# Single-column norm roots, grouped decay exponentials and separate value turning in a two-model block kernel

## The chip, the cores and the metric

The kernel runs on one core of a Trainium2 chip. The metric is the device time of one execution in microseconds. An execution of before is compared with one of after on the same inputs. Five engines work side by side: TensorE (PE, with its weight loads as PEld), VectorE (DVE), ScalarE (ACT), GpSimd (POOL) and SyncE (SP), which only issues DMAs here. Each takes its instructions in order from its own queue and waits at the head of the queue for semaphores of the others.

## The reference, cut to what matters

The program computes two blocks of two layers each on a sequence of 256 tokens, width 1024. The change touches the first layer's gated delta rule and the RMS norms in front of the layers.

```python
def rms_norm(x, gain):
    y = xf * lax.rsqrt(jnp.mean(xf * xf, axis=-1, keepdims=True) + NORM_EPS)
    return (y * gain)

def gdn_mixer(h, ...):
    proj = h @ w_in                      # q, k, v (4096 columns), z (2048), b, a (16 each)
    qkv = silu(causal_dwconv(qkv, conv_w))
    q, k = l2_norm(q), l2_norm(k)        # 8 heads of 128, each used by two of 16 value heads
    g = -exp(a_log) * softplus(a + dt_bias)
    o = gated_delta_rule(q, k, v, g, sigmoid(b))
    o = o * rsqrt(mean(o * o)) * out_gain * silu(z)
    return o @ w_out

# in gated_delta_rule, g summed up inside chunks:
    decay = where(tril, exp(g_i - g_j), 0)
    t_inv = inverse of (eye + strict lower part of k_beta k^T * decay)
    q_dec, k_dec = q * exp(g), k * exp(g_last - g)
```

## The kernel before

The program is unrolled and goes through stages: the gated delta rule (`gdn`, the first 330 us), a feed-forward layer, the second mixer, a second feed-forward layer, then the second model's two mixers and feed-forward layers. Each projection takes 512 KB chunks of weights. A chunk is loaded (`raw`, SP), split by ScalarE into a high part `wh` (a cast, L464) and by GpSimd or VectorE into the rest `wl` (a subtraction of `raw` and `wh`, L467 on GpSimd, L469 on VectorE; the letters P and V of `PLAN` say which, chunk by chunk). Three matmuls then stand for one exact product: `wh` with the high and the low part of the activations (L480, L492, L493) and `wl` with the high part (L483, L494). There are three slots for `raw` and three for `wh` and `wl`, so a chunk can't be prepared before the one three places ahead is done.

What order an engine's queue has is fixed ahead of time by the framework: it gives each instruction the rank that it has in the program, and lays out the queues by rank and by its own estimate of when operands are there. `issue_after(i)` puts the instructions of a block that run on i's engine behind i in that engine's queue, without a wait of its own.

**Norms.** `stats` (L547) sums the squares of a 128-token half by two ScalarE activations into two columns, and calls `rsqrt` (L496), which finds the root by an integer seed and three Newton steps on VectorE. For one column that is nine instructions: v (L505), seed (L509), -v/2 (L514), and three times t = (hv * y) * y (L517) and y = (t + 1.5) * y (L521); L505, L517 and L521 are `scalar_tensor_tensor`, with two tensor inputs in SBUF. `_norm` (L580 on) then makes the scaled rows (L582, `xn`, in the first norm `UU`: x times `rstd` times the row of gains), turns them by TensorE (L592, `ps_t`), and splits them into `h_hi` (L595, ScalarE) and `h_lo` (L596, VectorE). `stats` runs 14 times, twice in front of each of seven norms. The first norm stands at the start of the program, beside the first three weight chunks of z (`g_z`).

**Gated delta rule** (`_gdn_core`). In this order in the program: z of group 0 (`gates(0)`), the 32 columns b and a (`ps_ba`), the decays `gc` as cumulative sums and their turned copy `gcol` by TensorE (L840, L841), `gc` out to DRAM and back as `row`, broadcast over 128 partitions. Then `project` runs k's eight heads in four steps (`kp`) and q's in four (`qp`): per head 24 matmuls into `ps_g`, a causal convolution (`conv_silu`: ScalarE copy L738, three VectorE taps L740, Silu L741), a square `sq` (L868), and TensorE sums of the squares into `pss` (L855). After k's four steps the decays' differences are taken on VectorE (`ekd` L884, `GT` L886, 128x2048 each for two halves n), masked on GpSimd (L887) and exponentiated on ScalarE (L885, L888, L889). ScalarE holds the tables of one set of functions; between Exp and Silu the program has an `ACT_TABLE_LOAD`. Then k's roots (`rsqrt_p`), their turned copy `rrow` (L904) through DRAM into `row` again, the product with `GT` (L916), the matrix `UU` from `ps_kk` (L921 to L927), its diagonal blocks through DRAM into `sA`, and the triangular inverse of these on VectorE (`tri_inverse`, L1849 and L1850, 62 steps), whose result goes through DRAM into `TR`. Beside it the values' first group is projected.

What follows runs by a list of parts, `order`: v is a group of four value heads (`values`: project, convolve; then turn by TensorE, L965, `ps_v`, and multiply by beta, L966, into `vb`), z a group of gates, l the last two levels of the inverse, s the scan over the two halves with the output norm (`out_norm`, L1066 to L1072); parts with a plus run interleaved. The output projection starts beside s3.

Of the kernel before, what the change touches and what calls it, by code (L numbers as in the profile page):

```python
# [11 lines left out]
F32 = mybir.dt.float32  # L12
# [9 lines left out]
S = 256  # L22
# [19 lines left out]
        gk=4,  # L42
        order='v0 z1 v1 z2 l0 v2 l1+s0 v3 l2+s1 z3 l3+s2 s3',
# [337 lines left out]
class Prog:  # L381
    def __init__(self, ctx, tc, ap):
        self.tc, self.nc, self.ap = tc, tc.nc, ap
        nc = self.nc
        self.const = ctx.enter_context(tc.tile_pool(name="const", bufs=1, reuse_waits="tile"))
        self.xp = ctx.enter_context(tc.tile_pool(name="xp", bufs=1, reuse_waits="tile"))
        self.raw = ctx.enter_context(tc.tile_pool(name="raw", bufs=RAWB, reuse_waits="tile"))
        self.wsp = ctx.enter_context(tc.tile_pool(name="wsp", bufs=WSB, reuse_waits="tile"))
        self.hp = ctx.enter_context(tc.tile_pool(name="hp", bufs=1, reuse_waits="tile"))
        self.sm = ctx.enter_context(tc.tile_pool(name="sm", bufs=3, reuse_waits="tile"))  # L390
        self.pa = ctx.enter_context(tc.tile_pool(name="pa", bufs=4, space=PSUM, reuse_waits="tile"))
        self.dr = ctx.enter_context(tc.tile_pool(name="dr", bufs=1, space=DRAM))
# [8 lines left out]
        self.ada_held = None  # L401
        self.spare = []
# [69 lines left out]
    def mm3_a(self, ps, w, kt, width, m0, m, x):  # L472

        nc = self.nc
        (wh, wl), (xh, xl) = w, x
        n = 0
        last = 3 * kt - 1
        for k in range(kt):
            for xx in (xh, xl):
                nc.tensor.matmul(ps, wh[:, k * width + m0 : k * width + m0 + m], xx[:, k, :], start=(n == 0), stop=(n == last))  # L480
                n += 1
        for k in range(kt):
            nc.tensor.matmul(ps, wl[:, k * width + m0 : k * width + m0 + m], xh[:, k, :], start=False, stop=(n == last))  # L483
            n += 1
# [37 lines left out]

    def rsqrt_p(self, out, ws, n, eps, pool):
# [23 lines left out]
    def stats(self, x, t, junk):  # L547
# [6 lines left out]
        self.rsqrt(rstd, ss, (128, 1), 1.0, 1e-6)  # L554
# [178 lines left out]
    def conv_silu(self, pool, dst, ps, mt):  # L733

        nc = self.nc
        y = pool.tile([128, S], F32, name="cv_y", tag="cv_y", bufs=2)
        w = lambda i: self.fcol("convw", mt * 4 + i, 1)
        nc.scalar.activation(y, ps, AF.Copy, scale=w(3))  # L738
        for j in (1, 2, 3):
            nc.vector.scalar_tensor_tensor(y[:, j:], ps[:, : S - j], w(3 - j), y[:, j:], op0=ALU.mult, op1=ALU.add)  # L740
        self.last_conv = nc.scalar.activation(dst, y, AF.Silu)  # L741
# [19 lines left out]
    def _gdn_core(self, x, dr, gi, vb, rq, zs, inner):  # L761
# [42 lines left out]

        run(gates(0))
# [9 lines left out]
        with tc.tile_pool(name="g_r", bufs=1, reuse_waits="tile") as pr:  # L815
# [11 lines left out]
            na = pr.tile([16, 1], F32, name="na")  # L827
            nc.scalar.activation(na, self.fcol("alog", p1=16), AF.Exp)
            nc.vector.tensor_scalar(e, e, na, -1.0, op0=ALU.mult, op1=ALU.mult)
            on = self.one[0:16].to_broadcast([16, 128])  # L830
            gc = rt("gc")
# [5 lines left out]
            ps = self.pm.tile([128, 2, 2, 16], F32, name="ps_bg", tag="mm")  # L837
            for n in range(2):
                sl = slice(n * 128, n * 128 + 128)
                nc.tensor.transpose(ps[:, 0, n, :], beta[:, sl], self.ident[0:16, 0:16])  # L840
                nc.tensor.transpose(ps[:, 1, n, :], gc[:, sl], self.ident[0:16, 0:16])  # L841
            nc.vector.tensor_copy(cols, ps[:, 0])
            nc.vector.tensor_copy(gcol, ps[:, 1])
        sel = self.fcol("sel").rearrange("p (k m) -> p k m", k=8)

        def project(dst, c0, mt0, pool, tag):
# [11 lines left out]
            for c in range(4):  # L858
# [5 lines left out]
                for j in range(2):  # L864
# [3 lines left out]
                    nc.scalar.activation(sq, dst[:, k, :], AF.Square)  # L868
# [5 lines left out]
        with tc.tile_pool(name="g_rk", bufs=1, reuse_waits="tile") as pr:  # L874
            rrow = pr.tile([16, S], F32, name="rrow")
            kp, qp = project(kc, 0, 8, pe, "e"), project(qc, 4, 0, self.pm, "mm")
            for _ in range(self.plan["gk"]):
                next(kp)
            for n in range(2):
                row = pA.tile([128, 16, 128], F32, name="row", tag="row", bufs=2)  # L880
                nc.sync.dma_start(row, dg[:, n * 128 : n * 128 + 128].partition_broadcast(128))
                with tc.issue_after(self.last_conv.ins):
                    if n == 0:
                        nc.vector.tensor_tensor(ekd, row[:, :, 127], gcol[:, 0], op=ALU.subtract)  # L884
                        nc.scalar.activation(ekd, ekd, AF.Exp)  # L885
# [4 lines left out]
            for _ in range(4 - self.plan["gk"]):  # L890
                next(kp)
            next(qp)
            with tc.issue_after(self.last_raw.ins):
# [54 lines left out]

        def values(g):

            vt = []
            for c in range(2):
                ps = self.pa.tile([128, 2, S], F32, name="ps_g", tag="acc")
                v2 = gi.tile([128, 2, S], F32, name="v2", tag="v2", bufs=2)
# [6 lines left out]
                yield  # L961
            for n in range(2):
# [111 lines left out]
        G = dict(v=lambda g: values(g) if g else v0, l=levels, s=scan, z=gates)  # L1074
# [1175 lines left out]
```

## Time and profile before

| | us |
|---|---|
| median of three runs | 1586.95 (1583.37 to 1590.54) |
| profiled execution | 1586.77 |
| its span in the trace | 1585.1 |
| TensorE busy | 1452.5 (92%) |
| VectorE busy | 1124.0 (71%) |
| ScalarE busy | 817.5 (52%) |
| GpSimd busy | 663.6 (42%) |
| mean granted TensorE clock | 0.975 |

The span runs from the first to the last instruction of the trace; the profiled execution's time is 1.7 us more. A wait is the idle time of an engine in front of an instruction, named by what released it last. The granted clock is given as a share of 2.4 GHz. A matmul's duration in the trace is longer than the step to the next one, since they are pipelined. The trace's timeline merges neighbours of one kind: "x8" is eight instructions, with the time from the first one's start to the last one's end.

### The profile page before, as it was taken

To read this page: it belongs to the slowest core of one execution; us is meant where nothing else is said; L and a number is where in the kernel's file an instruction comes from. 1 tells how busy PE (TensorE), PEld (TensorE's weight loads), DVE (VectorE), ACT (ScalarE), POOL (GpSimd) and SP (SyncE) were. 2 spreads that over 40 slices of the span, in tenths; PEclk is the share of its full clock that TensorE was granted. 3 is DMA by queue.
4 is the path that set the end of the run, shared out by engine and by line. 5 is a ranking of instruction groups with operands and counts; after the bars stand their busy time and mean duration, and the time that the engine had idled before them with its cause. 6 is when DMAs were issued, how large, how long until landed. Compare 5 with 4: busy or idle time off the path is not lost.

```text
span 1585.1 us, 25794 instructions
## 1 busy us (share of the span) xinstructions
PE 1452.5 (92%) x9586; PEld 1285.2 (81%) x9586; DVE 1124.0 (71%) x2352; ACT 817.5 (52%) x1479; POOL 663.6 (42%) x433
## 2 busy tenths in 40 slices
PE   5788988999999899999998899898899889899998
PEld 4787877789988787999877676898887777589987
DVE  4567676769666766898476597799975768776652
ACT  4765544445343564554245475455444547466651
POOL 4445732236454241544136413266535521335630
PEclk9899999999999999999999999999999999999999
DMA  4555531478776454888533413777774441375551
GB/s 163 171 169 164 173 104 44 155 257 299 278 294 226 131 183 149 318 326 327 209 118 122 127 54 127 250 266 253 264 260 142 124 129 61 104 250 177 195 189 38
DMA packets 103246, 292.96 MB, mean 185 GB/s; under 512 B 28072, under 2 KB 37968, under 8 KB 96976
## 3 DMA queue, kind: packets, MB, share of 16 engines
q1 hardware_dynamic: 93872, 237.12, 44.3%
q10 hardware_dynamic: 8896, 53.14, 9.3%
q8 instruction: 75, 1.23, 0.3%
q0 software_dynamic: 352, 1.06, 0.2%
q14 instruction: 51, 0.42, 0.1%
HBM read 288.04 MB, written 3.24 MB: 184 GB/s over the span
## 4 chain that ended last, share of the span: by engine, by line
PE 50%; DVE 17%; DMA 5%; issue 4%; ACT 3%; POOL 2%; SPq 0%; ACTq 0%; DVEq 0%; POOLq 0%
PE ps_gu L480 13%; PE ps_gu L483 6%; PE ps_o L493 6%; PE ps_o L494 6%; PE ps_o L492 6%; DVE wl L469 4%; DVE ada_raw L1372 2%; DMA ada_raw<-in_ada 1%; DVE gu_u L2204 1%; ACT wh L464 1%; DMA raw<-in_u_gu 1%; POOL wl L467 1%; PE ps_u L480 1%; DVE rs_t L519 1%; PE ps_bs L1953 1%
## 5 line engine op out<-in xcount | busy, mean ns | idle before, releaser
L467 POOL TENSOR_TENSOR wl<-raw,wh 128x1024 fp32r<-128x1024 f32 (+4 forms) x162 | 403.6, 2498 | 425.6 <-ACT wh L464 344.3
L464 ACT CAST wh<-raw 128x1024 fp32r<-128x1024 f32 (+3 forms) x421 | 423.3, 1018 | 241.1 <-PE ps_o L493 91.1
L469 DVE TENSOR_TENSOR wl<-raw,wh 128x1024 fp32r<-128x1024 f32 (+2 forms) x259 | 347.6, 1352 | 134.4 <-ACT wh L464 132.6
L480 PE MATMUL ps_gu<-h_hi,wh 128*128 128x256 f32 x1280 | 312.6, 283 | 10.3 <-DVE gu_u L2204 10.3
L480 PE MATMUL ps_gu<-h_lo,wh 128*128 128x256 f32 x1280 | 312.0, 282 | 0.0
L480 PEld LDWEIGHTS ps_gu<-h_hi,wh 128*128 128x128 f32 x1280 | 244.2, 191 | 11.3 <-issue 9.0
L480 PEld LDWEIGHTS ps_gu<-h_lo,wh 128*128 128x128 f32 x1280 | 244.3, 191 | 0.2
L1372 DVE CUSTOM_DVE_ANT_0 ada_raw<-ada_raw,ada_cond 128x1024 f32<-128x1024 f32 x96 | 173.6, 1823 | 54.6 <-DMA ada_raw<-in_ada 54.5
L483 PE MATMUL ps_gu<-h_hi,wl 128*128 128x256 f32 x1280 | 178.5, 282 | 1.5 <-POOL wl L467 1.5
L483 PEld LDWEIGHTS ps_gu<-h_hi,wl 128*128 128x128 f32 x1280 | 163.7, 191 | 1.8 <-POOL wl L467 1.7
L494 PE MATMUL ps_o<-wl,act_h 128*128 128x512 f32 x352 | 139.0, 395 | 0.8 <-DVE wl L469 0.5
L493 PE MATMUL ps_o<-wh,act_l 128*128 128x512 f32 x352 | 138.6, 394 | 0.0
L492 PE MATMUL ps_o<-wh,act_h 128*128 128x512 f32 x352 | 138.4, 393 | 0.0
L2204 DVE SCALAR_TENSOR_TENSOR gu_u<-ps_gu,f2s,gu_u 128x254 f32<-128x254 f32 (+1 forms) x176 | 80.9, 477 | 41.2 <-ACT gu_u L2202 39.2
L725 POOL TENSOR_TENSOR act_l<-gu_t,act_h 128x256 fp32r<-128x256 f32 x44 | 55.6, 1267 | 112.8 <-ACT act_h L724 110.9
L2207 POOL TENSOR_TENSOR gu_t<-gu_t,gu_u 128x256 f32<-128x256 f32 x44 | 47.2, 1074 | 90.4 <-DVE gu_u L2204 87.0
L494 PEld LDWEIGHTS ps_o<-wl,act_h 128*128 128x128 f32 x352 | 66.1, 188 | 16.9 <-DVE wl L469 0.9
L493 PEld LDWEIGHTS ps_o<-wh,act_l 128*128 128x128 f32 x352 | 66.1, 188 | 15.1 <-issue 0.2
L492 PEld LDWEIGHTS ps_o<-wh,act_h 128*128 128x128 f32 x352 | 66.1, 188 | 14.9 <-issue 0.2
L2208 ACT CAST act_h<-gu_t 128x256 fp32r<-128x256 f32 x44 | 17.9, 407 | 101.9 <-POOL gu_t L2207 101.8
L740 DVE SCALAR_TENSOR_TENSOR cv_y<-ps_g,fi,cv_y 128x253 f32<-128x253 f32 (+2 forms) x96 | 44.9, 477 | 34.4 <-ACT cv_y L738 33.1
L480 PE MATMUL ps_g<-h_hi,wh 128*128 128x256 f32 x256 | 68.8, 301 | 0.0
(660 smaller groups left out, 3001.6 us busy)
## 6 DMA issues: line engine op xcount, KB each, us to landing
ada_raw<-in_ada ACTq DMA_DIRECT2D x48, 1024.0 KB, 6.3
raw<-in_f_gu SPq DMA_DIRECT2D x88, 512.0 KB, 4.6
raw<-in_u_gu SPq DMA_DIRECT2D x88, 512.0 KB, 4.3
raw<-in_f_dn SPq DMA_DIRECT2D x44, 512.0 KB, 4.7
raw<-in_u_dn SPq DMA_DIRECT2D x44, 512.0 KB, 4.2
raw<-in_g_qkv SPq DMA_DIRECT2D x32, 512.0 KB, 4.0
raw<-in_g_z SPq DMA_DIRECT2D x16, 512.0 KB, 4.0
raw<-in_g_out SPq DMA_DIRECT2D x16, 512.0 KB, 3.5
```

Of the source, the lines that this page charges most:

```text
L464: self.last_copy = nc.scalar.copy(wh[:, :cols], raw[:, :cols])
L467: nc.gpsimd.tensor_tensor(wl[:, :cols], raw[:, :cols], wh[:, :cols].bitcast(F32), op=ALU.subtract)
L469: nc.vector.tensor_tensor(wl[:, :cols], raw[:, :cols], wh[:, :cols].bitcast(F32), op=ALU.subtract)
L480: nc.tensor.matmul(ps, wh[:, k * width + m0 : k * width + m0 + m], xx[:, k, :], start=(n == 0), stop=(n == last))
L483: nc.tensor.matmul(ps, wl[:, k * width + m0 : k * width + m0 + m], xh[:, k, :], start=False, stop=(n == last))
L492: nc.tensor.matmul(ps, xh, wh[:, sl], start=start, stop=False, **kw)
L493: nc.tensor.matmul(ps, xl, wh[:, sl], start=False, stop=False, **kw)
L494: nc.tensor.matmul(ps, xh, wl[:, sl], start=False, stop=stop, **kw)
L725: nc.gpsimd.tensor_tensor(al[:, m, :], t, ah[:, m, :].bitcast(F32), op=ALU.subtract)
L1372: nc.vector.tensor_tensor_reduce(raw[:, j], raw[:, j], self.cond, 1.0, 0.0, op0=ALU.mult, op1=ALU.add, accum_out=mod[:, i : i + 1])
L2204: nc.vector.scalar_tensor_tensor(u[:, j, d:], ps[:, j, : S - d], cw[:, 3 * q + 2 - d : 3 * q + 3 - d], u[:, j, d:], op0=ALU.mult, op1=ALU.add)
L2207: nc.gpsimd.tensor_tensor(t, t, u[:, 0], op=ALU.mult)
```

## The change

It does three things. A new helper, `rsqrt_1`, replaces `rsqrt` in `stats`: the same nine steps, each a `tensor_scalar` with one tensor input, one column wide, whose other operands are one-column scalars per partition in SBUF. In the gated delta rule the turned decays are made after k's first step, the differences of the decays stand behind k's last convolution tap in VectorE's queue, and the exponentials `eg`, `ekd` and both `GT` stand together on ScalarE behind the last square of q's first step; later Silus of `conv_silu` stand behind them. The exponential of A_log moves to the front, and `gc` to a longer-lived buffer. Last, `values` is cut into `values` and `turned`, which `order` places one or more parts later; the buffers `v2` go from two to four.

```diff
-        gk=4,
-        order='v0 z1 v1 z2 l0 v2 l1+s0 v3 l2+s1 z3 l3+s2 s3',
+        order='v0 z1 t0 v1 z2 t1 l0 v2 l1+s0 t2 v3 l2+s1 t3 z3 l3+s2 s3',
...
+    def rsqrt_1(self, out, a, b, eps):
+        V = self.nc.vector
+        v, hv, t = (self.sm.tile([128, 1], F32, name=f"rs_{n}", tag=f"rs1_{n}") for n in "vht")
+        V.tensor_scalar(v, a, b, eps, op0=ALU.add, op1=ALU.add)
+        V.tensor_scalar(hv, v, -0.5, None, op0=ALU.mult)
+        seed = self.sm.tile([128, 1], I32, name="rs_s", tag="rs1")
+        V.tensor_scalar(seed, v.bitcast(I32), -0.5, float(0x5F3759DF), op0=ALU.mult, op1=ALU.add)
+        y = seed.bitcast(F32)
+        for i in range(3):
+            V.tensor_scalar(t, hv, y, y, op0=ALU.mult, op1=ALU.mult)
+            V.tensor_scalar(out if i == 2 else y, t, 1.5, y, op0=ALU.add, op1=ALU.mult)
...
-        self.rsqrt(rstd, ss, (128, 1), 1.0, 1e-6)
+        self.rsqrt_1(rstd, ss[:, 0:1], ss[:, 1:2], 1e-6)
...
-            nc.vector.scalar_tensor_tensor(y[:, j:], ps[:, : S - j], w(3 - j), y[:, j:], op0=ALU.mult, op1=ALU.add)
-        self.last_conv = nc.scalar.activation(dst, y, AF.Silu)
+            self.last_tap = nc.vector.scalar_tensor_tensor(y[:, j:], ps[:, : S - j], w(3 - j), y[:, j:], op0=ALU.mult, op1=ALU.add)
+        with self.tc.issue_after(self.behind.ins) if self.behind else ExitStack():
+            nc.scalar.activation(dst, y, AF.Silu)
...
+        na = gi.tile([16, 1], F32, name="na")
+        nc.scalar.activation(na, self.fcol("alog", p1=16), AF.Exp)
         run(gates(0))
...
-            gc = rt("gc")
+            gc = pA.tile([16, S], F32, name="gc")
...
             kp, qp = project(kc, 0, 8, pe, "e"), project(qc, 4, 0, self.pm, "mm")
-            for _ in range(self.plan["gk"]):
+            next(kp)
+            ps = self.pm.tile([128, 2, 2, 16], F32, name="ps_bg", tag="mm")
+            with tc.issue_after(self.last_mm.ins):
+                for n in range(2):
...
+                    nc.tensor.transpose(ps[:, 0, n, :], beta[:, sl], self.ident[0:16, 0:16])
+                    nc.tensor.transpose(ps[:, 1, n, :], gc[:, sl], self.ident[0:16, 0:16])
+            nc.vector.tensor_copy(cols, ps[:, 0])
+            nc.vector.tensor_copy(gcol, ps[:, 1])
+            for _ in range(3):
                 next(kp)
             for n in range(2):
                 row = pA.tile([128, 16, 128], F32, name="row", tag="row", bufs=2)
                 nc.sync.dma_start(row, dg[:, n * 128 : n * 128 + 128].partition_broadcast(128))
-                with tc.issue_after(self.last_conv.ins):
+                with tc.issue_after(self.last_tap.ins):
                     if n == 0:
                         nc.vector.tensor_tensor(ekd, row[:, :, 127], gcol[:, 0], op=ALU.subtract)
-                        nc.scalar.activation(ekd, ekd, AF.Exp)
                     nc.vector.tensor_tensor(GT[n], row, gcol[:, n].unsqueeze(2).to_broadcast([128, 16, 128]), op=ALU.subtract)
                 nc.gpsimd.affine_select(GT[n], GT[n], [[0, 16], [1, 128]], ALU.is_ge, -1e30, base=0, channel_multiplier=-1)
-                nc.scalar.activation(GT[n], GT[n], AF.Exp)
-            nc.scalar.activation(eg, gcol[:, 1], AF.Exp)
...
             next(qp)
+            with tc.issue_after(self.last_sq.ins):
+                nc.scalar.activation(eg, gcol[:, 1], AF.Exp)
+                nc.scalar.activation(ekd, ekd, AF.Exp)
+                for n in range(2):
+                    self.behind = nc.scalar.activation(GT[n], GT[n], AF.Exp)
...
         def values(g):
-            vt = []
+            vt = vts[g] = []
             for c in range(2):
...
-                v2 = gi.tile([128, 2, S], F32, name="v2", tag="v2", bufs=2)
+                v2 = gi.tile([128, 2, S], F32, name="v2", tag="v2", bufs=4)
...
                 vt.append(v2)
                 yield
+        def turned(g):
+            vt = vts.pop(g)
             for n in range(2):
                 ps = self.pm.tile([128, 4, 128], F32, name="ps_v", tag="mm")
```

## Rows read from the trace of the kernel before

**Rows 1.** Waits of TensorE, 0 to 330 us: total, times, longest (us).
```profile
PE pss L855 <- ACT sq L868: 8.1, 3, 5.3
PE ps_z L493 <- DVE h_lo L596: 6.9, 2, 6.7
PE ps_v L965 <- ACT v L741: 5.8, 3, 4.1
...
PE ps_kk L921 <- ACT kc L741: 1.8, 1, 1.8
...
PE ps_e L1723 <- DMA TR<-dTR: 1.2, 1, 1.2
```
**Rows 2.** Ten-us windows: length, busy (instructions) by engine, granted clock, DMA share, GB/s.
```profile
50.00:60.00 10.00, 10.00 (x88) 10.00 (x86) 7.03 (x10) 7.16 (x13) 7.54 (x3) 1.00 1.08 323
...
70.00:80.00 10.00, 4.66 (x22) 4.55 (x22) 3.78 (x9) 9.91 (x14) 2.47 (x2) 0.50 0.00 0
```
**Rows 3.** Timeline of VectorE: start, us, what, [idle before, releaser].
```profile
10.31 2.35 DVE L521 SCALAR_TENSOR_TENSOR rs_s<-rs_t,rs_s 128x1 f32<-128x1 f32 x1
...
17.75 0.75 DVE L582 SCALAR_TENSOR_TENSOR UU<-x_t,rstd,row 128x512 f32<-128x512 f32 x1
18.41 0.68 DVE L596 TENSOR_TENSOR h_lo<-ps_t,h_hi 128x512 fp32r<-128x512 f32 x1
...
148.31 0.69 DVE L966 TENSOR_TENSOR vb<-ps_v,bcol 128x512 f32<-128x512 f32 x1 [2.11 <-PE ps_v L965]
...
216.90 5.47 DVE L1072 SCALAR_TENSOR_TENSOR zs<-zs,g_rs,vb 128x128 f32<-128x128 f32 x4
```
**Rows 4.** Timeline of GpSimd, two places.
```profile
10.01 7.24 POOL L467 TENSOR_TENSOR wl<-raw,wh 128x1024 fp32r<-128x1024 f32 x3 [8.62 <-ACT wh L464]
...
953.77 0.64 POOL L1823 TENSOR_TENSOR a_Y<-a_Y,lay 128x256 f32<-128x256 f32 x1 [4.77 <-DVE rs_v L507]
```
**Rows 5.** Two lines of the code: count, ns min/median/max, first and last start (us).
```profile
L740 DVE SCALAR_TENSOR_TENSOR cv_y<-ps_g,fi,cv_y x96: 410/481/484, 46.9 to 228.3; 128x255 f32<-128x255 f32 x32, 128x254 f32<-128x254 f32 x32, 128x253 f32<-128x253 f32 x32
...
L517 DVE SCALAR_TENSOR_TENSOR rs_t<-rs_h,rs_s x54: 205/219/2260, 7.5 to 1390.7; 128x1 f32<-128x1 f32 x54
```
**Rows 6.** Timeline of VectorE, three places beside GpSimd's work.
```profile
279.87 2.25 DVE L509 TENSOR_SCALAR rs_s<-rs_v 128x4 int32<-128x4 int32 x1
...
332.75 3.58 DVE L582 SCALAR_TENSOR_TENSOR xn<-x_t,rstd,row 128x512 f32<-128x512 f32 x2
...
954.06 0.14 DVE L509 TENSOR_SCALAR rs_s<-rs_v 128x1 int32<-128x1 int32 x1
```
**Rows 7.** Timeline of TensorE.
```profile
19.15 0.80 PE L493 MATMUL ps_z<-wh,h_lo 128*128 128x512 f32 x1 [6.67 <-DVE h_lo L596]
...
24.55 1.03 PE L592 MATMUL ps_t<-ident,UU 128*128 128x128 f32 x8
...
77.58 0.56 PE L480 MATMUL ps_g<-h_hi,wh 128*128 128x256 f32 x1
...
86.07 0.51 PE L855 MATMUL pss<-fi,sq 128*128 128x16 f32 x4
```
**Rows 8.** Timeline of ScalarE around the exponentials.
```profile
64.95 1.91 ACT L888 ACTIVATE GT<-GT 128x2048 f32<-128x2048 f32 x1 [3.15 <-POOL GT L887]
66.88 1.28 ACT L741 ACT_TABLE_LOAD   x1
68.18 0.72 ACT L741 ACTIVATE kc<-cv_y 128x256 f32<-128x256 f32 x2
```
**Rows 9.** Timeline: a difference on VectorE, the two masks on GpSimd.
```profile
58.97 4.09 DVE L886 TENSOR_TENSOR GT<-row,gcol 128x2048 f32<-128x2048 f32 x1
...
60.86 6.02 POOL L887 TENSOR_SCALAR_AFFINE_SELECT GT<-GT 128x2048 f32<-128x2048 f32 x2
```
**Rows 10.** Timeline: the copy of rrow, its product with GT.
```profile
93.27 0.36 ACT L904 COPY rrow<-ps_rk 16x256 f32<-16x256 f32 x1 [1.20 <-PE ps_rk L903]
...
103.52 2.29 DVE L916 TENSOR_TENSOR row<-GT,row 128x2048 f32<-128x2048 f32 x1 [2.04 <-DMA row<-db]
```

More of the change, by code (lines that the diff above doesn't have):

```diff
@@ L401, in __init__ @@
         self.ada_held = None
+        self.behind = None
         self.spare = []
@@ L482, in mm3_a @@
         for k in range(kt):
-            nc.tensor.matmul(ps, wl[:, k * width + m0 : k * width + m0 + m], xh[:, k, :], start=False, stop=(n == last))
+            self.last_mm = nc.tensor.matmul(ps, wl[:, k * width + m0 : k * width + m0 + m], xh[:, k, :], start=False, stop=(n == last))
             n += 1
@@ L826, in _gdn_core @@
             nc.vector.scalar_tensor_tensor(e, xa, 0.0, e, op0=ALU.max, op1=ALU.add)
-            na = pr.tile([16, 1], F32, name="na")
-            nc.scalar.activation(na, self.fcol("alog", p1=16), AF.Exp)
             nc.vector.tensor_scalar(e, e, na, -1.0, op0=ALU.mult, op1=ALU.mult)
             on = self.one[0:16].to_broadcast([16, 128])
-            gc = rt("gc")
+            gc = pA.tile([16, S], F32, name="gc")
             for n in range(2):
@@ L836, in _gdn_core @@
             nc.sync.dma_start(dg, gc)
[L837 to L843, printed above, removed]
         sel = self.fcol("sel").rearrange("p (k m) -> p k m", k=8)
@@ L867, in project @@
                     sq = gi.tile([128, S], F32, name="sq", tag="sq", bufs=2)
-                    nc.scalar.activation(sq, dst[:, k, :], AF.Square)
+                    self.last_sq = nc.scalar.activation(sq, dst[:, k, :], AF.Square)
                     sqs.append((k, sq))
@@ L876, in _gdn_core @@
             kp, qp = project(kc, 0, 8, pe, "e"), project(qc, 4, 0, self.pm, "mm")
-            for _ in range(self.plan["gk"]):
+            next(kp)
+            ps = self.pm.tile([128, 2, 2, 16], F32, name="ps_bg", tag="mm")
+            with tc.issue_after(self.last_mm.ins):
+                for n in range(2):
+                    sl = slice(n * 128, n * 128 + 128)
+                    nc.tensor.transpose(ps[:, 0, n, :], beta[:, sl], self.ident[0:16, 0:16])
[3 more added lines that the diff above has]
+            for _ in range(3):
                 next(kp)
@@ L881, in _gdn_core @@
                 nc.sync.dma_start(row, dg[:, n * 128 : n * 128 + 128].partition_broadcast(128))
-                with tc.issue_after(self.last_conv.ins):
+                with tc.issue_after(self.last_tap.ins):
                     if n == 0:
                         nc.vector.tensor_tensor(ekd, row[:, :, 127], gcol[:, 0], op=ALU.subtract)
-                        nc.scalar.activation(ekd, ekd, AF.Exp)
                     nc.vector.tensor_tensor(GT[n], row, gcol[:, n].unsqueeze(2).to_broadcast([128, 16, 128]), op=ALU.subtract)
                 nc.gpsimd.affine_select(GT[n], GT[n], [[0, 16], [1, 128]], ALU.is_ge, -1e30, base=0, channel_multiplier=-1)
-                nc.scalar.activation(GT[n], GT[n], AF.Exp)
-            nc.scalar.activation(eg, gcol[:, 1], AF.Exp)
-            for _ in range(4 - self.plan["gk"]):
-                next(kp)
             next(qp)
+            with tc.issue_after(self.last_sq.ins):
[3 more added lines that the diff above has]
+                    self.behind = nc.scalar.activation(GT[n], GT[n], AF.Exp)
             with tc.issue_after(self.last_raw.ins):
@@ L947, in _gdn_core @@
             nc.sync.dma_start(dTR[1], A.rearrange("p c j -> p (c j)"))
+        vts = {}
         def values(g):
-            vt = []
+            vt = vts[g] = []
             for c in range(2):
                 ps = self.pa.tile([128, 2, S], F32, name="ps_g", tag="acc")
-                v2 = gi.tile([128, 2, S], F32, name="v2", tag="v2", bufs=2)
+                v2 = gi.tile([128, 2, S], F32, name="v2", tag="v2", bufs=4)
                 for j in range(2):
@@ L1072, in out_norm @@
                     nc.vector.scalar_tensor_tensor(zs[n][g][:, u, :], zs[n][g][:, u, :], rs[:, u : u + 1], o[:, u, :], op0=ALU.mult, op1=ALU.mult)
-        G = dict(v=lambda g: values(g) if g else v0, l=levels, s=scan, z=gates)
+        G = dict(v=lambda g: values(g) if g else v0, t=turned, l=levels, s=scan, z=gates)
         *first, last = self.plan["order"].split()
```

## The prediction

> **What bounds the kernel now.** The page's busy times come first (the table above): TensorE works nearly throughout, so time can be won only where it stands idle or runs at its lower clock. The diff touches the gated-delta-rule stage (the first 330 us) and the norm roots of all stages. For that stretch I read the waits of TensorE, sorted by their sum [rows 1], then ten-us windows [rows 2] to see what a wait costs afterwards: in 50 to 60 us TensorE is busy throughout at clock 1.00 (2.4 GHz) with 88 matmuls, in 70 to 80 us for 4.66 us with 22, and its granted clock is 0.50 (1.2 GHz). Three waits belong to the three parts of the change: 6.9 us for h_lo of the first norm, 8.1 us for the squares sq (longest 5.3), 5.8 us for v (longest 4.1). Last, I read the queues of the other engines around each of the three, to see what ends the wait.
>
> **Part 1, the roots.** In the first norm VectorE's one-column root steps, normally about 0.22 us for the slower kind [rows 5], take up to 2.35 us: the step at 10.31, and two like it at 12.70 and 15.00 [rows 3]. Each ends when one of the three GpSimd subtractions that begin at 10.01 (2.4 us apiece) ends [rows 4]. They have two tensor inputs in SBUF. Behind them in VectorE's queue stand UU (17.75) and h_lo (18.41), and TensorE waits for h_lo. The new steps read one tensor; the rest are per-partition scalars. Does a one-input step wait? The 96 convolution taps, one input in PSUM, one in SBUF and a scalar, never took over 0.484 us [rows 5], though GpSimd subtracts beside many; a one-column tensor_scalar at 954.06 took 0.14 us in the middle of a GpSimd tensor_tensor (953.77 to 954.41) [rows 4, 6]. The same op on four columns took 2.25 us at 279.87 [rows 6], so columns matter, and the new ones are single.
>
> The Trainium skill, "SBUF — State Buffer", section "Who interferes with whom", speaks against this part: tensor_scalar may enter a mode that takes the port shared with GpSimd, and is then blocked for a whole instruction. The row at 279.87 agrees for four columns, the one at 954.06 does not for one. By the rule alone part 1 would be worth nothing (second rival).
>
> What is late next: the two remaining UU steps (x times rstd times row, two SBUF inputs) wait as before; such a pair took 3.58 us beside GpSimd at 332.75, 1.5 when free [rows 6]. So: five steps of about 0.2 end at 11.4 instead of 17.7; UU waits for the first subtraction (12.6) and ends at 13.4; h_lo's first half (0.68) at 14.1, against 19.1. The second UU waits for the second subtraction (13.4 + 2.4 = 15.8), h_lo's second half ends at 17.2, the third subtraction at 16.5 + 2.4 = 18.9. TensorE restarts at 14.1 instead of 19.15, needs that third split from about 18, and finishes its last four matmuls at 19.8 instead of 24.55 [rows 7]: **4.7 us**. Ends: 2.3 (one more subtraction, 2.4 us, in the way) and 6 (UU does not wait). Everything behind it is a chain from h_lo (z, ba, decays, weights by slots), so it moves as a whole. The other twelve roots run the same number of steps, nine; with 0.14 to 0.22 us for one [rows 5, 6] each changes by -0.3 to +0.2 us: I take 0, ends -3 and +2 for all. The early exponential of A_log is one short activation moved ahead in ScalarE's queue; taken at 0, with up to 1 us if it waits for its DMA in front of a cast.
>
> **Part 2, the exponentials.** Now each GT exponential (1.91 us) sits between k's activations with a table load of 1.28 us on either side (one stands in the rows), and the first waits 3.15 us for GpSimd's mask [rows 8]. The squares come late, TensorE waits, then works at the low clock. What goes: the 5.3 us wait for sq and the 1.8 us for kc [rows 1], and the low clock behind them: q's first pair, 48 matmuls, takes from 77.58 to 86.07, 8.5 us [rows 7], where 88 matmuls, a few small sums among them, fill 10 us at full clock [rows 2], so about 5.8 for 48 with their sums; 2.7 us too much. Together 9.8 us by 86.07. Five of ten table loads between 36 and 91 us go too (6.4 us of ScalarE), covered there by TensorE's work.
>
> What comes: after q's first pair ScalarE does load, eg, ekd, GT twice, load: 1.28 + 0.4 + 3.8 + 1.28 = 6.8 us in one piece. Queued behind it are the next Silus, weight casts, and the copy of rrow, for which the whole chain to the triangular inverse waits. q's pair would end at 86.1 - 9.8 = 76.3; its convolution (three taps of 0.48 and three short activations, about 3 us) at 79.3; the exponentials end at 86.1. GT must be there: the subtractions (2.3 us as the equal-sized product in [rows 10], one took 4.09 beside GpSimd) now follow k's last tap (about 68: 76.3 less the pair's 5.8 and the kk products and sums in front) and end at 73 to 76; the masks (3.0 each) at 79 to 82 with a weight split between [rows 9]. So rrow goes from 93.27 to about 86.9, and its product with GT from 103.52 to about 97 [rows 10]: the chain wins **6.4 us**, not 9.8, and TensorE, in order, waits for the rest at kk. Ends: 0 (masks behind two more splits, rrow no earlier) and 9.8. Casts behind the 6.8 us block are covered by three weight slots, each some 2.9 us of matmuls (half of the pair's 5.8); without that cover the block costs up to 4 us, which lies inside these ends. The transposes of the decays behind a named matmul lose a short wait and meet gc, which comes no earlier: 0.
>
> The Trainium skill, "ScalarE: Activation LUTs", section "What ACT_TABLE_LOAD costs", counts a drain of 1.38 us beside each load, 2.66 in all. Here the load at 66.88 begins as the exponential ends, and the next activation starts at 68.18, 1.30 later [rows 8]: no such drain. By the page the block would be 2.8 us longer and the part worth 3.6.
>
> **Part 3, turning apart from projecting.** TensorE's waits for v go (5.8 us), but what stands behind each decides. VectorE waits 2.11 us at 148.31 for ps_v in the middle of the triangular inverse [rows 3], 2.8 us with a second such place; TensorE waits 1.2 us for the inverse's result TR [rows 1]. Both move, so about 1.5 us is won by the first level step. The longest wait, 4.1 us before 226, hides a VectorE stretch: four steps of the output norm took 5.47 us from 216.90 beside GpSimd [rows 3], and the scan behind them starts no earlier; TensorE would do the z matmuls there and miss them later. I take 0 of it, ends 0 and 4. Part 3: **1.5 us**, ends 0 and 5.
>
> **Sum.** 4.7 + 6.4 + 1.5 = 12.6 us off the profiled execution of 1586.77 us (span 1585.1 and 1.7 around it), which lies within 0.2 us of the median of the three runs, 1586.95: **1574.2 us**.
>
> **Rivals.** First, the gain of part 2 is given back: rrow is no earlier because the GT masks stand behind weight splits in GpSimd's queue, and TensorE arrives early at TR and waits. For it: TensorE already waits 1.2 us there. Against: q's end moves the inverse too. It gives 1586.8 - 4.7 = 1582. Second, the new one-column steps wait for GpSimd as the old ones: 1586.8 - 7.9 = 1578.9; only the rule speaks for it. Third, all covers hold: 6 + 9.8 + 5 = 20.8, 1566. Fourth, slower: between 200 and 300 us the output norms' two-input and four-column steps meet GpSimd's splits, each meeting worth 2.25 us [rows 6]; I count ten now. The shifted order can meet more often. If part 2 is also lost, three more meetings use up part 1's 4.7, and six make it slower by 13.5 - 4.7 = 8.8: 1595.6. For it: nothing orders these engines against each other. Against: six more on ten is much for an unchanged stretch.
>
> **How the numbers follow.** Forecast 0.57, rivals 0.20, 0.05, 0.12 and 0.06. Within 0.5% means 7.9 us, about what a measurement of this kernel can tell from no change, so from 1578.8 on it is no change. Faster: 0.53 of the forecast, the third rival, half of the second: 0.68. Slower: the fourth and a little: 0.07. Same: 0.25. The range goes from the third rival's 1566 to 1584, which takes in the first rival; the slow case and both tails, under 0.2, stay out.
>
> **What would show it.** Right: no one-column root step over 0.3 us near 10 us and TensorE back at its matmuls at about 14; no wait for sq over 2 us and clock 1.00 between 60 and 90; five table loads there; rrow some 11 us earlier (both parts); no wait for v. Wrong: 2.3 us steps left at 10 us; ScalarE idle in front of the GT exponentials with casts behind it; a longer wait for TR; a longer stretch from TR to the end of the stage.

## The result, and the profile after

| | before | after |
|---|---|---|
| median, four runs each side by side (us) | 1585.89 (1583.37 to 1590.54) | 1563.95 (1560.75 to 1570.74) |
| profiled execution | 1586.77 | 1570.74 |
| its span | 1585.1 | 1569.0 |
| first level step (ps_e) starts | 190.21 | 188.16 |
| last output product of the first stage starts | 326.06 | 301.10 |

A level step is a matmul of the inverse's last two levels; the first one (`ps_e`) needs the inverse's result TR. The last output product is the last matmul of the first stage's output projection (`ps_o`).

The change is faster: ratio 0.9866, 95% interval 0.9841 to 0.9891, some 21 us. The forecast of 1574.2 and its range from 1566 to 1584 were too high. The profiled execution of after took the longest of its four, so its trace shows only 16.1 us of the gain. In the traces 25 us are won by the end of the first stage, 18.1 are left when the next stage's gate-up matmuls begin (343.53 before, 325.43 after), 16.1 at the end.

The waits of TensorE in the first 330 us of after (us in total, times, longest):
```profile
PE ps_t L605 <- DVE UU L595: 11.9, 2, 10.0
PE ps_t L605 <- DVE xn L595: 5.6, 3, 2.1
PE ps_z L493 <- DVE h_lo L609: 4.8, 2, 4.6
PE ps_bg L891 <- DVE gc L848: 3.1, 1, 3.1
...
PE ps_e L1745 <- DMA TR<-dTR: 0.5, 1, 0.5
```
The waits for sq, kc and v of [rows 1] are gone. The wait for h_lo has shrunk to 4.6 us, but one for UU of 1.8 has appeared ahead of it (the 10.0 is the program's start), and the next norm's xn costs 5.6 (2.0 in before, from 326 to 346 us).

Windows of after (length; busy us and instructions of PE, PEld, DVE, ACT and POOL; granted clock; DMA share and GB/s):
```profile
36.00:100.00 64.00, 59.25 (x461) 58.21 (x459) 40.95 (x70) 43.80 (x75) 39.54 (x16) 0.92 0.62 195
100.00:190.00 90.00, 87.65 (x607) 80.31 (x605) 75.02 (x163) 53.25 (x102) 65.38 (x31) 1.00 0.67 201
...
70.00:80.00 10.00, 10.00 (x87) 10.00 (x87) 9.89 (x9) 5.13 (x10) 6.77 (x3) 1.00 0.50 158
```
The same windows of before:
```profile
36.00:100.00 64.00, 52.17 (x386) 50.86 (x385) 34.41 (x64) 46.53 (x75) 34.56 (x14) 0.87 0.55 171
100.00:190.00 90.00, 80.36 (x550) 73.99 (x548) 65.74 (x151) 47.13 (x88) 53.31 (x27) 0.96 0.60 179
```
From 70 to 80 us TensorE is now busy throughout at clock 1.00, where [rows 2] has 4.66 us at 0.50. From 36 to 190 us it is busy 14.4 us longer (7.1 + 7.3), at a higher clock.

ScalarE of after, the exponentials together:
```profile
87.48 1.28 ACT L906 ACT_TABLE_LOAD   x1
88.77 0.22 ACT L906 ACTIVATE eg<-gcol 128x16 f32<-128x16 f32 x1
...
89.00 3.69 ACT L909 ACTIVATE GT<-GT 128x2048 f32<-128x2048 f32 x2
92.60 0.34 ACT L921 COPY rrow<-ps_rk 16x256 f32<-16x256 f32 x1
```
The exponentials stand together as forecast, but they begin late (the forecast had the block at 79.3, without part 1), and rrow behind them comes at 92.60 where [rows 10] has 93.27: 0.7 us earlier, not the 11 forecast for both parts together. Part 2 by itself was to bring 6.4 of these; in exps_alone (below) rrow comes at 90.83, 2.4 earlier. The block stands behind q's first squares, which end at 87.46, and these need q's convolution taps. In VectorE's queue the taps stand behind the differences that feed GT, and these met GpSimd's subtractions:
```profile
73.28 2.16 DVE L901 TENSOR_TENSOR ekd<-row,gcol 128x16 f32<-128x16 f32 x1
75.36 6.69 DVE L902 TENSOR_TENSOR GT<-row,gcol 128x2048 f32<-128x2048 f32 x2
81.97 0.47 DVE L753 SCALAR_TENSOR_TENSOR cv_y<-ps_g,fi,cv_y 128x255 f32<-128x255 f32 x1
```
GpSimd's second mask stands behind a weight split, but ends at 88.25, ahead of the first GT exponential at 89.00:
```profile
86.24 2.01 POOL L903 TENSOR_SCALAR_AFFINE_SELECT GT<-GT 128x2048 f32<-128x2048 f32 x1
```
So where do 25 us come from, if the chain to the inverse wins next to nothing? TensorE's projections behind the first level step tell it. Before, from 190.2 to 263 us (count, busy us, mean ns):
```profile
L492 PE MATMUL ps_z<-wh,h_hi 128*128 128x512 f32 x16 | 6.8, 427 | 0.0
L493 PE MATMUL ps_z<-wh,h_lo 128*128 128x512 f32 x16 | 6.8, 426 | 0.0
L494 PE MATMUL ps_z<-wl,h_hi 128*128 128x512 f32 x16 | 6.8, 426 | 0.0
L480 PE MATMUL ps_g<-h_hi,wh 128*128 128x256 f32 x25 | 6.7, 297 | 0.0
L480 PE MATMUL ps_g<-h_lo,wh 128*128 128x256 f32 x26 | 6.7, 286 | 0.0
...
L483 PE MATMUL ps_g<-h_hi,wl 128*128 128x256 f32 x32 | 5.0, 288 | 0.0
```
After, from 188.1 to 240 us; there is no ps_g among them:
```profile
L492 PE MATMUL ps_z<-wh,h_hi 128*128 128x512 f32 x6 | 2.6, 427 | 0.0
L493 PE MATMUL ps_z<-wh,h_lo 128*128 128x512 f32 x6 | 2.5, 410 | 0.0
L494 PE MATMUL ps_z<-wl,h_hi 128*128 128x512 f32 x6 | 2.4, 394 | 0.0
```
Before, 83 products ps_g and 48 ps_z stand behind the first level step; after, 18 ps_z. Undisturbed, 96 ps_g took 11.68 us (152.10 to 163.78 of before), 48 ps_z 11.1 (145.88 to 156.96 of after): 0.12 and 0.23 us each, so 21 us stood behind it and 4 stand there now. From the first to the last level step it takes 72.4 us before, 51.1 after; from there to the end of the stage 63.4 and 61.9.

### The profile page after: what moved, and what is told of

Its sections match the earlier page's. It is cut to its first block, busy times and chain, and to the rows that moved or that the text cites. A ratio compares the mean times of both kernels' runs of the same rounds, so it can differ in the third digit from the quotient of the medians.

```text
span 1569.0 us, 25783 instructions
## 1 busy us (share of the span) xinstructions
PE 1455.1 (93%) x9586; PEld 1286.3 (82%) x9586; DVE 1120.2 (71%) x2352; ACT 811.7 (52%) x1474; POOL 659.3 (42%) x433
## 5 line engine op out<-in xcount | busy, mean ns | idle before, releaser
L469 DVE TENSOR_TENSOR wl<-raw,wh 128x1024 fp32r<-128x1024 f32 (+2 forms) x259 | 356.9, 1385 | 145.2 <-ACT wh L464 143.2
L1394 DVE CUSTOM_DVE_ANT_0 ada_raw<-ada_raw,ada_cond 128x1024 f32<-128x1024 f32 x96 | 160.5, 1685 | 68.7 <-DMA ada_raw<-in_ada 68.7
L738 POOL TENSOR_TENSOR act_l<-gu_t,act_h 128x256 fp32r<-128x256 f32 x44 | 51.8, 1179 | 102.7 <-ACT act_h L737 102.7
L480 PE MATMUL ps_g<-h_lo,wh 128*128 128x256 f32 x256 | 66.2, 293 | 0.0
```

The lines of the kernel that those rows point to most:

```text
L469: nc.vector.tensor_tensor(wl[:, :cols], raw[:, :cols], wh[:, :cols].bitcast(F32), op=ALU.subtract)
L738: nc.gpsimd.tensor_tensor(al[:, m, :], t, ah[:, m, :].bitcast(F32), op=ALU.subtract)
L1394: nc.vector.tensor_tensor_reduce(raw[:, j], raw[:, j], self.cond, 1.0, 0.0, op0=ALU.mult, op1=ALU.add, accum_out=mod[:, i : i + 1])
```

## The experiments

Each was timed in five rounds beside the kernel before. "Left" is the projection work behind the first level step, counted as above; "f0" is the time from the gate-up norm's first xn to that of the next norm, "last" from the last norm's first xn to the end, all from the traces (us).

| kernel | ratio, 95% interval | first level step | left | last output product | f0 | last |
|---|---|---|---|---|---|---|
| before | 1 | 190.2 | 21 | 326.1 | 189.3 | 197.6 |
| after (1+2+3) | 0.9866, 0.9841 to 0.9891 | 188.2 | 4 | 301.1 | 194.2 | 202.7 |
| roots_alone (1) | 1.0025, 1.0006 to 1.0044 | 187.8 | 21 | 323.5 | 192.8 | 200.2 |
| exps_alone (2) | 0.9849, 0.9827 to 0.9871 | 187.7 | 4 | 300.3 | 189.0 | 197.5 |
| turn_alone (3) | 0.9946, 0.9926 to 0.9966 | 188.9 | 22 | 320.0 | 188.5 | 197.5 |
| no_roots (2+3) | 0.9823, 0.9794 to 0.9853 | 186.8 | 4 | 299.1 | 188.2 | 197.5 |
| no_turn (1+2) | 0.9848, 0.9817 to 0.9879 | 188.9 | 4 | 300.8 | 192.3 | 200.6 |
| no_exps (1+3) | 0.9969, 0.9950 to 0.9987 | 184.5 | 22 | 315.7 | 192.4 | 202.7 |
| exps_pure | 0.9840, 0.9818 to 0.9863 | 189.6 | 4 | 304.9 | 188.0 | 197.2 |
| order_alone | 0.9934, 0.9915 to 0.9953 | 215.7 | 0 | 318.8 | 188.1 | 197.4 |
| lo_first | 0.9884, 0.9863 to 0.9904 | 184.4 | 4 | 299.3 | 193.1 | 203.6 |
| first_only | 0.9894, 0.9862 to 0.9926 | 183.3 | 4 | 297.7 | 194.9 | 199.4 |
| roots_rest | 1.0050, 1.0030 to 1.0071 | 190.6 | 21 | 326.5 | 196.0 | 201.2 |
| rest_f0v | 1.0045, 1.0023 to 1.0066 | 189.2 | 21 | 324.9 | 191.4 | 198.7 |
| first_v | 0.9782, 0.9760 to 0.9804 | 182.1 | 4 | 294.9 | 188.2 | 197.3 |
| after_first_v | 0.9830, 0.9802 to 0.9857 | 183.5 | 4 | 296.9 | 193.2 | 200.7 |
| first_v_f0v | 0.9803, 0.9776 to 0.9831 | 182.4 | 4 | 296.7 | 189.1 | 197.2 |

**One part alone, and one part undone.** roots_alone, exps_alone and turn_alone put the change's hunks on the kernel before, one part each; no_roots, no_turn and no_exps leave one out. By their main lines:
```diff
# roots_alone: this alone; no_roots: this undone
-        self.rsqrt(rstd, ss, (128, 1), 1.0, 1e-6)
+        self.rsqrt_1(rstd, ss[:, 0:1], ss[:, 1:2], 1e-6)
# exps_alone / no_exps
-                nc.scalar.activation(GT[n], GT[n], AF.Exp)
...
+            with tc.issue_after(self.last_sq.ins):
# turn_alone / no_turn
-        order='v0 z1 v1 z2 l0 v2 l1+s0 v3 l2+s1 z3 l3+s2 s3',
+        order='v0 z1 t0 v1 z2 t1 l0 v2 l1+s0 t2 v3 l2+s1 t3 z3 l3+s2 s3',
```


> The kernel before with the roots of part 1 alone. Theory: the wait on GpSimd only moves to the two-input UU steps behind the roots, and h_lo of the first half stands behind UU of the second in VectorE's queue, so TensorE restarts at about 19.1 us as before; ratio 1.000, 1584 to 1588 us. Rival, the forecast: TensorE restarts at 14.1 and the kernel gains 4.7 us, about 1581, ratio 0.997.

> The kernel before with part 2 alone (exponentials together, transposes of the decays moved). Theory: projections are a store of work that fills whatever TensorE time is freed ahead of TR, so all of the idle time and half-clock time taken out between 36 and 100 us comes off the end of the stage: about 7 us of idle time and 3 us of clock, some 10 us, 1576 us, ratio 0.9937. Rival: only what brings TR forward counts, and rrow is less than 1 us earlier: 1 to 2 us, 1584. The forecast had 6.4, 1579.5.

> The kernel before with part 3 alone (values turned apart from projecting). Theory of the store of work: TensorE's waits for v (5.8 us) and the half-clock time behind them go and the later scans run without projections between: 7 us, 1579, ratio 0.9956. Rival, the forecast: 1.5 us, 1584.5, ratio 0.999; a second rival is that it gains only where part 2 has freed time: 0, 1586.

> The changed kernel with the old roots (parts 2 and 3 without part 1). If the parts add up (exponentials alone 24 us, turning alone 8.6), 1554 us, ratio 0.979. Theory of the store of work: the exponentials' part has used up the projections that were left behind TR, so turning has nothing more to give: 1559 to 1562, ratio 0.983, TR again near 188 us and the stage's last output product at about 300.

> The changed kernel without part 3 (roots and exponentials). Theory: roots cost 3 to 4 us and turning gives nothing behind the exponentials: 1564 to 1566, ratio 0.987, equal to the changed kernel. Rival, the parts add: 1572, ratio 0.991.

> The changed kernel without part 2 (roots and turning). Both theories: plus 4 and minus 8.6, about 1582, ratio 0.997; the forecast's terms would give 1586.8 - 6.2 = 1580.6.

On the 1587 us of before, the roots alone cost 4 us, the exponentials win 24, the turning wins 8.6. The exponentials alone are worth as much as the whole change. The parts don't add: 28.6 us in sum, 21 together. Turning is worth 8.6 us on before, and about as much on the kernel with the roots (no_exps beside roots_alone), but 4 beside the exponentials (no_roots against exps_alone, intervals overlap) and nothing that can be told in the whole change (no_turn against after). All of the exponentials' expectations were too small, the theory's 10 us too. roots_alone is slower than both of its expectations; its first stage is faster nevertheless, and the loss lies behind it (see the norms below).

**Which piece of part 2.** exps_pure leaves the decays' transposes, gc and the exponential of A_log where they were:
```diff
-        na = gi.tile([16, 1], F32, name="na")
-        nc.scalar.activation(na, self.fcol("alog", p1=16), AF.Exp)
...
-            next(kp)
-            with tc.issue_after(self.last_mm.ins):
...
+            for _ in range(4):
```


> Part 2 with the exponentials together only: the decays' transposes and the exponential of A_log stay where they were. Theory: the exponentials are all of it: 1561 to 1565, ratio 0.985. Rival: the late transposes, which take a TensorE wait out of the stretch, bring a quarter or more: 1568 to 1572, ratio 0.989.

0.9840 beside 0.9849: the place of the exponentials, and of the differences that feed them, is all of it.

**Freed time or order.** With the exponentials together, TensorE's queue has 17 us more projection ahead of the first level step. order_alone puts all 21 us ahead of it without freeing time:
```diff
-        order='v0 z1 v1 z2 l0 v2 l1+s0 v3 l2+s1 z3 l3+s2 s3',
+        order='v0 z1 v1 z2 v2 v3 z3 l0 l1+s0 l2+s1 l3+s2 s3',
...
+        with self.tc.issue_after(behind.ins) if behind else ExitStack():
             for u in range(8):
```


> The kernel before, with only the order of TensorE's work changed: all value and gate projections are issued ahead of the first level step (131 matmuls, some 21 us, stand behind it in the kernel before, 18, some 4 us, in the three kernels with the exponentials together). Theory: it is TensorE's freed time that pays, not the order; without that time the first level step comes at 203 to 210 us, from there to the last level step it takes about 50 instead of 72, and the two cancel: 1582 to 1588, ratio 0.997 to 1.0. Rival: TensorE has room ahead of TR, and the order alone brings most of the 24 us: first level step by 195, 1565 to 1572, ratio 0.988.

Its windows:
```profile
36.00:100.00 64.00, 52.55 (x395) 51.07 (x394) 33.87 (x64) 46.96 (x75) 34.88 (x14) 0.89 0.53 172
100.00:190.00 90.00, 81.90 (x540) 75.92 (x539) 65.53 (x150) 45.43 (x86) 53.27 (x27) 0.92 0.58 178
190.00:215.60 25.60, 24.23 (x155) 21.36 (x155) 12.30 (x23) 12.62 (x21) 16.66 (x8) 1.00 0.63 169
```
Its first level step, which waits for nothing but its queue:
```profile
215.68 0.70 PE L1724 MATMUL ps_e<-TR,UU 128*32 128x32 f32 x32
```
The first level step comes 25.5 us later than before; from it to the last it takes 41.2 us for 72.4. The net, 10.5 us by the ratio (7.3 at the last output product), is more than the theory's 0 to 5 and far from the 24 of the rival. It has a place: TensorE's idle time between first and last level step falls from 10.0 to 4.1 us, and the longest wait for v (4.1) is among what goes. The same stretches of exps_alone:
```profile
36.00:100.00 64.00, 59.30 (x468) 58.39 (x467) 41.66 (x70) 45.46 (x80) 40.53 (x16) 0.95 0.64 197
100.00:187.70 87.70, 84.73 (x583) 76.86 (x582) 69.56 (x156) 48.96 (x90) 61.82 (x30) 1.00 0.67 201
```
From 36 us to its first level step TensorE stands idle for 21.7 us in before, 20.9 in order_alone and 7.7 in exps_alone, at a mean clock of 0.92, 0.92 and 0.98. So the order is worth some 6 to 10 us, about what turning brings alone; the rest of the exponentials' gain needs the freed time.

**The first norm.** lo_first adds one order to the changed kernel; first_only goes back to the old roots in all other norms, too; first_v is no_roots with the stage's first four splits on VectorE, and after_first_v has the new roots as well:
```diff
# lo_first, first_only
+                        with self.tc.issue_after(lo.ins) if t and first else ExitStack():
                             nc.vector.scalar_tensor_tensor(xn[:, hv], ...
# first_v, after_first_v
-        w='PPPVPPPPPVPP...
+        w='VVVVPPPPPVPP...
```


> The changed kernel with one order more: in the first norm the UU steps of the second half of x are issued behind h_lo of the first half. Theory, that the queue order was what kept part 1 from paying: h_lo of the first half ends near 14.5 us, TensorE restarts there instead of 19.05, and 3 to 5 us come off: about 1560 against 1564, ratio to the kernel before 0.9835. Rival: the second half ends later by as much as the first gains, and the projections need both: within 1 us of the changed kernel's 1564.

> The changed kernel with the new roots in the first norm alone, the old ones in the other norms, and UU of the second half of x behind h_lo of the first. Theory: the new roots cost time in the other norms (the first gate-up norm and the last one took some 4 and 5 us longer in each of the three kernels that have them) because the planned order around them shifts; without them there 1567.7 comes down by 8 to 11 us: 1557 to 1560, ratio 0.982. Rival: those 9 us are an accident of when weight splits fall, and the kernel stays within 2 us of 1567.

> Parts 2 and 3 with the old roots, and the first four weight splits of the stage on VectorE instead of GpSimd, so that nothing runs beside the first norm. Theory: the one-column steps take 0.2 us and UU 0.75, TensorE is back at 14 to 15 us instead of 19, TR comes 3 us earlier and the end with it: 1557 to 1559, ratio 0.981. Rival: the chain behind TR gives it back, as two us of lo_first's four were: 1560 to 1562, ratio 0.983.

> The changed kernel with the first four weight splits on VectorE instead of GpSimd. Theory: the first norm then pays with old or new roots alike (TensorE back at about 13), and the new roots still cost 4 to 8 us in the other norms: 1559 to 1563, ratio 0.982, against 0.978 for the same kernel with the old roots. Rival: the cost of the new roots came with the meeting in the first norm: 1555, ratio 0.978.

In after, VectorE's steps stand beside GpSimd's subtractions from 9.98 to 17.84 so:
```profile
9.99 2.90 DVE L595 SCALAR_TENSOR_TENSOR UU<-x_t,rstd,row 128x512 f32<-128x512 f32 x1
12.81 0.20 DVE L534 TENSOR_SCALAR rs_s<-rs_t,rs_s 128x1 f32<-128x1 f32 x1
13.05 0.27 DVE L533 TENSOR_SCALAR rs_t<-rs_h,rs_s 128x1 f32<-128x1 f32 x1
...
13.61 4.79 DVE L595 SCALAR_TENSOR_TENSOR UU<-x_t,rstd,row 128x512 f32<-128x512 f32 x2
18.31 1.28 DVE L609 TENSOR_TENSOR h_lo<-ps_t,h_hi 128x512 fp32r<-128x512 f32 x2
```
lo_first, same engine and place:
```profile
9.96 0.74 DVE L597 SCALAR_TENSOR_TENSOR UU<-x_t,rstd,row 128x512 f32<-128x512 f32 x1
...
13.18 1.29 DVE L611 TENSOR_TENSOR h_lo<-ps_t,h_hi 128x512 fp32r<-128x512 f32 x2 [1.79 <-ACT h_hi L610]
14.38 1.40 DVE L597 SCALAR_TENSOR_TENSOR UU<-x_t,rstd,row 128x512 f32<-128x512 f32 x1
```
TensorE's first matmul with h_lo in after:
```profile
19.05 0.80 PE L493 MATMUL ps_z<-wh,h_lo 128*128 128x512 f32 x1 [4.56 <-DVE h_lo L609]
```
In lo_first:
```profile
13.92 0.79 PE L493 MATMUL ps_z<-wh,h_lo 128*128 128x512 f32 x1
```
The one-column steps wait no longer; the wait went into UU, with h_lo behind both UU of the second half. roots_alone has that order too, but there the second UU begins just ahead of GpSimd's first subtraction (10.08):
```profile
9.86 0.74 DVE L595 SCALAR_TENSOR_TENSOR UU<-x_t,rstd,row 128x512 f32<-128x512 f32 x1
```
TensorE goes on with h_lo at 16.77 there, and the first level step comes 2.4 us earlier than in before: the first norm wins something alone, and next to nothing in after. With h_lo ahead (lo_first), TensorE goes on with h_lo at 13.92 and the first level step comes 3.8 us earlier than in after, but only 1.8 are left at the end of the stage, and later stages run slower: one, from its norm on, takes 184.2 us for 174.0, though none of its code was touched. VectorE's order differs there too: of some 485 instructions about 340 keep the sequence that they have in after, where no_roots keeps 469 and takes 173.2 us. So a planned order shifts far behind an edit; that the shift makes the ten us is argued, no run has it alone. first_only has the same 184.8 there, with an order as different, so its expectation fell, and neither kernel prices the roots. first_v keeps all it wins: TensorE at 13.06, first level step 4.6 us and last output product 4.2 us earlier than no_roots. At 0.9782 it is the best version, 13 us below the changed kernel; with the new roots it is 0.9830.

**The roots in the other norms.** roots_rest has the new roots in all norms but the first; rest_f0v then moves two splits of the gate-up norm to VectorE, and first_v_f0v does that to first_v:
```diff
-        w='PPVVVPPVPVV...
+        w='PPVVVVVVPVV...
```


> The kernel before with the new roots in all norms but the first. Theory: the loss lies in these norms (the gate-up norm's stage 192.8 us against 189.3, the last 200.2 against 197.6), and what the first norm won (TR 2.4 us earlier) is missing here: 1590 to 1594, ratio 1.003 to 1.004. Rival: the new roots cost nothing by themselves and the loss comes with the shift of the first stage: 1587, ratio 1.000.

> The kernel with the new roots in all norms but the first, and the two weight splits that GpSimd makes beside the second pair of UU steps of the gate-up norm moved to VectorE; the order around them is else the same. Theory, that the new roots lose by where they put that pair (it stands behind a second split and beside both of GpSimd's, and takes 5.4 us for 3.6): the pair takes 1.5 us, one more split of 1.2 stands ahead of it, h_lo comes 2 to 3 us earlier, TensorE keeps its full clock, and the gate-up stage takes 190 to 192 us for 196.0; kernel 1591, ratio 1.0015. Rival, that it is the longer steps of the roots themselves (0.4 us a root) and nothing of the meeting: the stage stays at 195 to 197, ratio 1.005.

> Parts 2 and 3 with the old roots, the first four splits of the first stage on VectorE, and the two splits beside the gate-up norm's second pair too. With the old roots that pair meets one split only (3.6 us), so 2 us are to be had and one more VectorE split (1.2 us) is paid: 1554, ratio 0.977; if the lower clock behind the wait is saved too, 1552.

VectorE of roots_rest, the gate-up norm's second pair:
```profile
334.74 1.22 DVE L469 TENSOR_TENSOR wl<-raw,wh 128x1024 fp32r<-128x1024 f32 x1
...
336.11 5.38 DVE L598 SCALAR_TENSOR_TENSOR xn<-x_t,rstd,row 128x512 f32<-128x512 f32 x2
```
GpSimd beside it:
```profile
335.44 5.50 POOL L467 TENSOR_TENSOR wl<-raw,wh 128x1024 fp32r<-128x1024 f32 x2 [12.51 <-ACT wh L464]
```
VectorE of rest_f0v:
```profile
334.25 1.41 DVE L598 SCALAR_TENSOR_TENSOR xn<-x_t,rstd,row 128x512 f32<-128x512 f32 x2
```
With the new roots VectorE has two splits ahead of that pair (before: one, with the second behind it) and both of GpSimd's beside it: 5.4 us, where [rows 6] has 3.58. Without the meeting the pair takes 1.4 and the stage 191.4 us for 196.0, as expected: that shows what the meeting does to the pair. The stage's time is read from one execution of each kernel, of 1587.2 and 1601.0 us, and the medians did not follow: 1595.6 and 1596.5, ratios 1.0045 and 1.0050, both above what the theories had (1.0015, and 1.003 to 1.004). So the meeting explains the gate-up stage in the profiled executions, and no run prices it on the kernel. first_only, with the old roots in this norm, takes 194.9 us for the stage, so the new roots are not the only way into such an order.

The traces show a second place, the last norm: "last" is 197.2 to 197.6 us with the old roots (first_only: 199.4), 198.7 to 203.6 with the new ones. In after, and in roots_alone too, the planned order puts a weight split of VectorE, stretched beside one of GpSimd, ahead of both h_lo of the second half, and TensorE waits. After, VectorE and TensorE:
```profile
1378.37 2.05 DVE L469 TENSOR_TENSOR wl<-raw,wh 128x1024 fp32r<-128x1024 f32 x1 [1.39 <-ACT wh L464]
1380.35 1.28 DVE L609 TENSOR_TENSOR h_lo<-ps_t,h_hi 128x512 fp32r<-128x512 f32 x2
...
1381.08 0.80 PE L493 MATMUL ps_gt<-wh,h_lo 128*128 128x512 f32 x1 [1.59 <-DVE h_lo L609]
```
no_roots, VectorE and TensorE:
```profile
1374.97 0.69 DVE L609 TENSOR_TENSOR h_lo<-ps_t,h_hi 128x512 fp32r<-128x512 f32 x1 [0.93 <-ACT h_hi L608]
...
1375.71 0.50 PE L493 MATMUL ps_gt<-wh,h_lo 128*128 128x512 f32 x1
```
TensorE's mean clock in 20 us from about there on (1376.3 and 1373.6) is 0.83 in after and 1.00 in no_roots. One stage seems to give some back: the one whose norm stands at 967 us in after (990 in before) takes 211.4 to 216.6 us in the kernels with the new roots there and 215.6 to 224.2 in the others.

What the new roots cost the kernel as a whole stays open: it is 4 us alone, 7 in the whole change (after against no_roots; the intervals overlap), 8 in after_first_v against first_v, and nothing in no_turn against exps_alone. Their own steps are longer: nine follow each other in 2.2 us (the first three from 306.03 to 306.53 of after, the other six from 300.96 to 302.62), the old nine in 1.8 (0.45 for the first three and 0.45 for each of three pairs, exps_alone); over twelve roots that would be up to 5 us, an estimate that no run has by itself. first_v_f0v is no better than first_v: with the old roots the move gains nothing.

## Why the prediction was too high

**Part 2 is where it failed: 6.4 us forecast, 24 measured.** What goes was right: no wait for sq or kc, clock 1.00 in the window from 70 to 80, five table loads. What comes was wrong twice. rrow comes 2.4 us earlier with part 2 alone and 0.7 in the whole change, not 6.4 and 11: ekd and the two differences, 8.8 us of VectorE in one piece (71.50 to 80.27 in exps_alone; forecast from 68 to between 73 and 76), kept q's taps and squares, and so the block, waiting. And it did not matter, because the step behind it failed: that the part is worth what the chain to the inverse wins, and "TensorE, in order, waits for the rest at kk". That chain takes the same time in both, 96.9 us from rrow to the first level step in before (93.27 to 190.21) and in exps_alone (90.83 to 187.71). Its two ends in exps_alone, on ScalarE and TensorE:
```profile
90.83 0.34 ACT L921 COPY rrow<-ps_rk 16x256 f32<-16x256 f32 x1
187.71 0.22 PE L1740 MATMUL ps_e<-TR,UU 128*32 128x32 f32 x2 [0.39 <-DMA TR<-dTR]
```
Its end in before:
```profile
190.21 0.22 PE L1723 MATMUL ps_e<-TR,UU 128*32 128x32 f32 x2 [1.25 <-DMA TR<-dTR]
```
TensorE fills that time with projections, of which before leaves 21 us behind it and exps_alone 4. Time freed ahead takes from that: 17 us of matmuls moved, 2.5 us by the earlier TR, 3.4 us less idle time among the level steps (10.0 to 6.6), 22.9 in sum, of 25.8 at the last output product. The missing 2.9 are not told apart; the clock among the level steps goes from 0.93 to 1.00. The row that gave it away stood in the trace of before: the ps_g and ps_z behind the first level step.

**Part 1: 4.7 us forecast, a loss of some 4 alone.** The first link was right: single-column steps with pointers don't wait (0.20 to 0.27 us beside a subtraction). The next one took VectorE's order from before: one UU, h_lo, the second UU. The changed kernel has both UU ahead of both h_lo, and UU waits as [rows 6] said. With the order of the forecast (lo_first) TensorE is back at 13.92, where the forecast had 14.1. And the other norms, put at 0 with up to 2 us of loss, cost more than that (roots_rest: 0.5%, 8 us). The Trainium skill, "SBUF — State Buffer", section "Who interferes with whom", says that tensor_scalar can enter a mode that contends with GpSimd, if its operands meet certain conditions. These one-column steps did not contend; UU, with two SBUF inputs, is the one that waits.

**Part 3: 1.5 us forecast, 8.6 alone.** The waits for v went, as said. The first level step comes 1.3 us earlier, close to the 1.5. "I take 0 of it" for the 4.1 us behind 216.90 was wrong: idle time among the level steps falls from 10.0 to 5.4 us in turn_alone, much as in order_alone. The two make 5.9 of the 6.1 us at the last output product; the profiled execution shows no more of the 8.6, and whether the two further buffers `v2` have a share is not told apart. Beside part 2, which leaves nothing but 18 products there, about 4 or none are left.

**The rivals.** The first had rrow right, which hardly comes earlier, but not what holds it (the differences, not the masks) nor what follows: TensorE waits 0.5 us for TR, where [rows 1] has 1.2. The third, all covers hold, had the right direction and 20.8 us, near the measured 21, by luck: it counts 6 us for roots that lose and 9.8 for exponentials that win 24. The second fell with the steps of 0.2 us. Of the fourth, the meetings of output norms did not decide; that the roots lose by meetings in other norms is its mechanism in another place.

## What to carry to other kernels

Before a gain is capped by the chain that it feeds, count the independent work that the engine still has behind that chain's end: as long as there is some, freed time ahead of the chain's end pays beyond what the chain itself wins, and what two changes can free draws on the same store. A wait that is taken from one instruction goes to the next one of its queue that has the same conflict; taking away the other side (here the splits on GpSimd) paid in the first norm (first_v), while in the gate-up norm the same move brought nothing that the kernel's time shows. Where a planner orders the queues, an edit's order has to be read from the new program, and stages that the edit does not touch have to be compared by their own durations.

## What was not expected of the hardware

Which of two conflicting instructions begins first decides by tenths of a microsecond: UU at 9.96 us, ahead of a subtraction that began at 10.20 (lo_first), took 0.74 us; UU at 9.99, behind one that began at 9.98 (after), took 2.90. The pairs of roots_alone (9.86 ahead of 10.08: 0.74) and first_only (10.13 behind 9.93: 2.70) agree. Size alone did not protect: the tensor_tensor of 128x16 at 73.28 took 2.16 us beside a subtraction from 73.00 to 75.40, where the tensor_scalar of 128x1 at 12.81 took 0.20.
